# Thirty-two conditioning tiles of a two-layer block: loaded and multiplied in layer 1 instead of layer 0

## The chip, the core and the metric

The kernel runs on one core of a Trainium2 chip. The metric is the device time of one execution in microseconds, and lower is better. Five engines each work through their own instructions in order: TensorE (PE in the profile; PEld is its weight loads), VectorE (DVE), ScalarE (ACT), GpSimd (POOL) and SyncE (SP, which here only issues DMAs).

## What is computed

A block of two layers works on 1024 latent rows and 256 context rows of width 1024. Each layer has a token mixer (an HGRN recurrence, a windowed attention and an RG-LRU, side by side) and a convolved FFN. Each layer is conditioned by six vectors of 1024: shift, scale and gate of the mixer and of the FFN. They come from one matrix product per layer, and this product is what the change moves:

```python
for layer in range(DEPTH):
    want_ctx = layer < DEPTH - 1
    mod = sc @ ada_w[layer] + ada_b[layer]
    mod_c = scc @ ada_w[layer] + ada_b[layer]
    sh1, sc1, g1, sh2, sc2, g2 = jnp.split(mod, 6, axis=-1)
    ...
    h_l = modulate(x, norm_mix_g[layer], sh1, sc1)
    y_l, y_c = token_mixer(h_l, h_c, w_in[layer], w_out[layer], ...)
    x = x + g1[:, None, :] * y_l
    x = x + g2[:, None, :] * conv_ffn(modulate(x, norm_ffn_g[layer], sh2, sc2), ...)
```

So `sh1` and `sc1` of layer 1 are needed before that layer's mixer starts, while its other four vectors are needed only after the mixer.

## The kernel before

**Conditioning tiles.** `ada_w` of one layer is 1024 x 6144. `ada_gen(l, t)` (L183) makes one third of it, 2048 columns, in 16 tiles of 128 x 1024 (512 KB each). A tile is one load into a buffer named `aw` (L190, issued on SP) and four matmuls of 256 columns into the PSUM tile `ada` (L199). After the sixteenth tile, one copy on ACT (`adaev`, L205), four transposes (`adat`, L208) and two additions on DVE end the third. `ada_step` (L366) multiplies the tile that was loaded last and starts the load of the next. The third (0, 0) is made at the start; five thirds, 80 tiles, stand in a list and are made one tile at a time beside other work. A tile's buffer is taken from the weight rings named in `aring`: `wd`, or `wd` and `wr` in turn. Each of these two rings has a single buffer.

**Where the steps stand.** In layer 0 every projection of the mixer (`proj`, L557) has two steps, one behind each half of the latent rows: 16 projections, 32 tiles. Layer 0's attention (`att_step`, L1065) has 20 more. The remaining 28 stand in layer 0's FFN: `up` (L1260; its matmuls are `pu` for the latent rows, `puc` for the context rows) loads one ahead of each of its column tiles and multiplies it behind. Layer 1 has none.

**Weights of a projection.** `load_w` (L321) loads 512 KB into the single buffer of `wr` (L325), then ACT casts the high part (`wh`, L315) and DVE subtracts to get the low part (`wl`, L316); `wh` and `wl` have two buffers each. A projection is 48 matmuls of 512 columns into `pl` and, where context rows are wanted, 24 of 256 columns into `pc` (both L341).

**The HGRN stage.** For each of two head pairs, `hg_in` makes three projections and `hg_scan` (L638) works through groups of rows. Layer 1 reads out two groups, of 512 rows each, per scan. A group takes one score step and seven levels; each level copies operands on ACT (`ks` L690, `qz` L663), runs eight score matmuls (`hd`, L668; sixteen records in the trace), merges them on DVE (L692), and updates `Q` and `K` on DVE (L703, L705). Behind the levels stand `ho` (L719), transposes `kt` (L728, copied by ACT in L729), `kv` (L736), a chain on DVE over the chunks (L754) and `hi` (L765). Then come the readout `hg_out` with its normalization (L235 to L238, logarithm and exponential on ACT), the gates (`gs`, a sigmoid on ACT, L781) and the RG-LRU (`pg`, L833). The attention follows, with its queries and keys (`rot`, `q`), scores (`sc`) and so on.

**What sets the order.** The code is written stage after stage, but a scheduler lays out every engine's order from dependencies, priorities and free buffers when the program is built. A projection of a later stage can thus be laid between the instructions of an earlier one as soon as its weights have a buffer.

Of the kernel before, what the change touches and what calls it, by code (L numbers as in the profile page):

```python
# [87 lines left out]
def tile_dit(ctx: ExitStack, tc: tile.TileContext, x, c, ctxt, c_ctx, ada_w, ada_b, norm_mix_g, norm_ffn_g,  # L88
# [262 lines left out]
    adas = []  # L351
# [14 lines left out]
    def ada_step():  # L366

        ada_mm()
        ada_load()
# [91 lines left out]
        aring[1] += 1  # L461
        return wtile(aring[0][aring[1] % len(aring[0])], "aw", F32, 1)

    adas += [ada_gen(l_, t_, ada_tile) for l_, t_ in ((0, 1), (0, 2), (1, 0), (1, 1), (1, 2))]
    porder = InOrder(tc, POOL_ENGINE)
    with porder:
        G.tensor_copy(out=tiny("pj", [P, 1], 1), in_=last_raw[:, 0, 0:1])
# [82 lines left out]
    def mixers(l, hl, hc, steps):  # L550
# [6 lines left out]
        def proj(srcs, lat=True, cx=True):  # L557
            wh, wl = pre.pop() if pre else load_w(*srcs)
            pl = pc = None
            if lat:  # L560
                pl = ps("pl")
                for b in (B0, B1):
                    mm3(pl[:, b], wh, wl, *cut(hl, b))
                    ada_step()
            if cx:
                pc = pb1("pc")[:, 0:C]
                mm3(pc, wh, wl, *cut(hc, BC))
            return pl, pc
# [69 lines left out]
        def hg_scan(p, F2, K2, qp):  # L638
# [9 lines left out]
            for g in (1, 2, 0):  # L648
# [34 lines left out]
                Tm = f2  # L683
                m = 1
                for li in range(7):
                    nm_ = w // m
                    nb = nm_ // 2
                    if hasq and m < 64:
# [85 lines left out]
        def hg_gate(p):  # L774

            pl, pc = pr(O_G + p * P, cx=want)
            gsl = L("gs")
            gs = [X("gsc") if want else None, gsl[:, B0], gsl[:, B1]]
            for o_, a in zip(gs, (pc, pl[:, B0], pl[:, B1])):
                if a is not None:  # L780
                    S.activation(out=o_, in_=a, func=AF.Sigmoid)  # L781
                    V.scalar_tensor_tensor(out=o_, in0=a, scalar=rows["hn"][:, 2 * l + p:2 * l + p + 1], in1=o_, op0=mult, op1=mult)
            return gs
# [103 lines left out]
        def act(**kw):  # L887
            with order:
                S.activation(**kw)

        lrus = [lru(p) for p in range(2)]
        oSs = [hg_scan(0, *hg_in(0))]
        gin = hg_in(1)
        gate = hg_gate(0)
        oSs.append(hg_scan(1, *gin))
        gate = [gate, hg_gate(1)]
        hg_out(0, gate[0])
        hg_out(1, gate[1])
        for st in "c0 g0 c1 k0 s0 y0 o0 g1 k1 s1 y1 o1".split():
# [165 lines left out]
        def att_step(s_):  # L1065
# [14 lines left out]
                    done.add((qb, kv))  # L1080
            if pvs and pvs[0][0] <= s_:
                att_pv(*pvs.pop(0)[1:])
            if l == 0 and s_ % 2 and s_ < 4 * len(grp) - 40:
                ada_step()

        outs = []
# [33 lines left out]
            s_ += 1  # L1120
        ada_mm()
        aring[0] = ["wd"]
        if l == 0:
            ada_fin(0, 1)
        for i_, a in yr.items():
            hi, lo = L("yah", F32R), L("yal", F32R)
            split(hi, lo, a)
# [576 lines left out]
    for l in range(DEPTH):  # L1704
# [32 lines left out]
            sums7(xl, tb, n1)  # L1737
        next(f_)
        if want:
            for w_ in range(2):  # L1740
                ada_fin(1, w_)

            def after(si, xa):
                for mh, th in {1: [(0, 0)], 4: [(1, 1)], 5: [(1, 0)], 6: [(0, 1)]}.get(si, []):
# [53 lines left out]
```

## Time and profile before

| | |
|---|---|
| median of 3 runs | 3042.76 us (3041.82 to 3046.66) |
| profiled execution, its own time | 3040.61 us |
| its span, first to last instruction | 3038.8 us |
| PE busy | 2880.4 us, 95% |
| DVE, ACT, POOL busy | 1901.4, 1421.5, 236.6 us |
| tile `ada`, matmul records | 768 (96 tiles, 8 each) |
| granted clock, mean | 0.978 |

Times of the trace count from the first instruction. Layer 0's HGRN stage begins near 145 us, its attention near 490, its output projection at 669, its FFN at 789. Layer 1 begins near 1720 us; its first scan runs from 1812 to 1867 us, its second from 1895 to 1957, its attention from 2078 to about 2230. A busy PE means that one of its matmuls is in flight; it does not mean that all its columns do work.

### The profile page before, as it was taken

What the parts mean: (1) busy time and instruction counts of PE and PEld (TensorE: products, weight loads), DVE (VectorE), ACT (ScalarE), POOL (GpSimd) and SP (SyncE); (2) the same over time, 40 slices, a digit from 0 to 9 for tenths busy, and PEclk for the clock granted to TensorE, in tenths of its full rate; (3) what the DMA queues carried; (4) which work ended last, traced back from release to release, by engine and by line L of the source; (5) the groups of instructions that cost most, each with busy time, mean ns of one, the idle gap of its engine ahead of it and who ended that gap; (6) DMA issues with size and microseconds to landing.
All of it is one profiled execution on the core that took longest, in us unless ns stands there. A gap on an engine that the chain in (4) does not pass through costs nothing.

```text
span 3038.8 us, 41813 instructions
## 1 busy us (share of the span) xinstructions
PE 2880.4 (95%) x16208; PEld 2275.7 (75%) x16208; DVE 1901.4 (63%) x3005; ACT 1421.5 (47%) x2445; POOL 236.6 (8%) x348
## 2 busy tenths in 40 slices
PE   6999898999999999999999899998998999998998
PEld 5867676558888888888878787675666788876776
DVE  5466556665644434444676756767747777776876
ACT  5366764663422222222334545785745545544343
POOL 2000002000000000000101000002010111112010
PEclk9999999999999999999999999999998899999998
DMA  7211246423333223222476200114053333336762
GB/s 296 69 60 53 67 132 187 115 98 121 96 100 102 87 96 94 72 71 82 175 249 174 93 28 22 36 63 108 11 170 91 79 95 97 97 95 220 239 188 90
DMA packets 286678, 335.75 MB, mean 110 GB/s; under 512 B 19180, under 2 KB 211856, under 8 KB 286480
## 3 DMA queue, kind: packets, MB, share of 16 engines
q1 hardware_dynamic: 242928, 231.29, 24.6%
q0 software_dynamic: 43376, 101.73, 11.2%
q8 instruction: 128, 2.10, 0.3%
q14 instruction: 70, 0.57, 0.1%
q10 hardware_dynamic: 176, 0.07, 0.0%
HBM read 276.65 MB, written 56.36 MB: 110 GB/s over the span
## 4 chain that ended last, share of the span: by engine, by line
PE 76%; DVE 8%; ACT 7%; DMA 6%; issue 2%; SPq 0%; POOL 0%; ACTq 0%; DVEq 0%; POOLq 0%
PE pu L341 16%; PE pl L341 9%; PE ux L1445 8%; PE px L1651 5%; PE py L1651 4%; PE puc L341 4%; PE uz L1445 3%; PE iv L587 3%; PE yo L1160 3%; PE sc L1005 3%; PE yo L1154 2%; DMA raw<-in_ffn_w_down_dram 2%; PE pov L1047 2%; PE pt L1030 2%; PE pc L341 2%
## 5 line engine op out<-in xcount | busy, mean ns | idle before, releaser
L1445 PE MATMUL ux<-t,sw 128*128 128x512 f32 x1320 | 320.6, 399 | 20.1 <-ACT t L315 10.5
L1445 PEld LDWEIGHTS ux<-t,sw 128*128 128x128 f32 x1320 | 248.3, 190 | 85.3 <-ACT t L315 13.1
L341 PE MATMUL pu<-hh,wh 128*128 128x512 f32 x704 | 278.7, 396 | 0.1
L341 PE MATMUL pu<-hh,wl 128*128 128x512 f32 x704 | 276.3, 393 | 0.0
L341 PE MATMUL pu<-hl,wh 128*128 128x512 f32 x704 | 275.1, 391 | 0.0
L1278 DVE SCALAR_TENSOR_TENSOR u<-pu,col_fcb,u 128x1023 f32<-128x1023 f32 x44 | 56.3, 1282 | 324.5 <-ACT u L1277 324.5
L315 ACT CAST wh<-wr 128x1024 fp32r<-128x1024 f32 x110 | 115.2, 1049 | 227.7 <-PE pc L341 66.5
L341 PE MATMUL pl<-hh,wh 128*128 128x512 f32 x512 | 210.4, 411 | 2.2 <-ACT wh L315 0.9
L341 PE MATMUL pl<-hh,wl 128*128 128x512 f32 x512 | 205.2, 401 | 1.0 <-DVE wl L316 1.0
L341 PE MATMUL pl<-hl,wh 128*128 128x512 f32 x512 | 204.8, 400 | 0.0
L1277 ACT ACTIVATE u<-pu,col_nf,col_fcw 128x1024 f32<-128x1024 f32 x44 | 53.0, 1206 | 318.0 <-PE pu L341 318.0
L316 DVE TENSOR_TENSOR wl<-wr,wh 128x1024 fp32r<-128x1024 f32 x110 | 135.9, 1236 | 67.4 <-ACT wh L315 61.9
L315 ACT CAST ah<-raw 128x512 fp32r<-128x512 f32 x132 | 76.2, 619 | 200.2 <-PE py L1651 99.9
L341 PEld LDWEIGHTS pu<-hh,wh 128*128 128x128 f32 x704 | 132.2, 188 | 38.3 <-issue 11.4
L341 PEld LDWEIGHTS pu<-hh,wl 128*128 128x128 f32 x704 | 132.3, 188 | 29.0 <-issue 0.4
L341 PEld LDWEIGHTS pu<-hl,wh 128*128 128x128 f32 x704 | 132.2, 188 | 28.0 <-issue 0.2
L1445 PE MATMUL uz<-t,sw 128*128 128x512 f32 x528 | 132.6, 398 | 0.0
L341 PEld LDWEIGHTS pl<-hh,wh 128*128 128x128 f32 x512 | 96.1, 188 | 35.3 <-issue 14.0
L1445 PEld LDWEIGHTS uz<-t,sw 128*128 128x128 f32 x528 | 100.6, 191 | 23.4 <-ACT t L315 0.9
L1011 DVE TENSOR_REDUCE st<-sc 128x1 f32<-128x641 f32 (+2 forms) x144 | 106.7, 745 | 17.8 <-ACT sc L1010 16.3
L1014 ACT ACTIVATE pb<-sc,st 128x641 f32<-128x641 f32 (+2 forms) x144 | 106.3, 739 | 20.7 <-DVE st L1011 18.0
L341 PEld LDWEIGHTS pl<-hh,wl 128*128 128x128 f32 x512 | 96.2, 188 | 26.1 <-issue 5.1
(464 smaller groups left out, 7357.3 us busy)
## 6 DMA issues: line engine op xcount, KB each, us to landing
raw<-in_ffn_w_down_dram SPq DMA_DIRECT2D x220, 256.0 KB
aw<-in_ada_w_dram SPq DMA_DIRECT2D x96, 512.0 KB
wr<-in_ffn_w_up_dram SPq DMA_DIRECT2D x44, 512.0 KB
b<-act POOLq DMA_DIRECT2D x35, 512.0 KB, 8.0
wr<-in_w_in_dram SPq DMA_DIRECT2D x34, 512.0 KB
act<-u POOLq DMA_DIRECT2D x66, 256.0 KB, 3.5
wr<-in_w_out_dram SPq DMA_DIRECT2D x128, 128.0 KB
dr<-in_ffn_w_down_dram SPq DMA_DIRECT2D x22, 512.0 KB
```

What stands on the lines that cost most here:

```text
L315: S.copy(out=hi, in_=raw)
L316: eng.tensor_tensor(out=lo, in0=raw, in1=hi.bitcast(F32), op=sub)
L341: PE.matmul(out=o, lhsT=wl[k] if pi == 2 else wh[k], rhs=hl[k] if pi == 1 else hh[k], start=(k == 0 and pi == 0), stop=(k == nk - 1 and pi ...
L587: PE.matmul(out=po[:, 0:384], lhsT=hh[1 if pi == 1 else 0][k][:, t0:t0 + P], rhs=wiv[k][1 if pi == 2 else 0], start=(k == 0 and pi == 0), ...
L1005: PE.matmul(out=o_, lhsT=qt[:, hh, :], rhs=k_[:, ksl], start=(pi == 0), stop=(pi == 1 and not ms))
L1011: V.tensor_reduce(out=st[:, 0, c_], in_=sc[:, s0:769], axis=mybir.AxisListType.X, op=ALU.min)
L1014: S.activation(out=pb, in_=sc[:, s0:769], func=AF.Exp, bias=st[:, 0, c_], scale=-1.0, accum_out=st[:, 1, c_])
L1030: PE.transpose(out=pt[:, hh * P:(hh + 1) * P], in_=pbs[qb, kv][hh][:, i * P:(i + 1) * P], identity=ident)
L1047: PE.matmul(out=pov[hsl(v_), :], lhsT=vt(kbs[i])[:, hsl(v_)], rhs=ptss[qb][i][:, v_, :], start=(i == 0), stop=(i == nk - 1))
L1160: PE.matmul(out=o, lhsT=wl[k] if pi == 2 else wh[k], rhs=a[1 if pi == 1 else 0][:, s_], start=False, stop=(ki == 3 and pi == 2), skip_grou ...
L1445: PE.matmul(out=out, lhsT=(al if pi == 2 else ah)[:, k * P:(k + 1) * P], rhs=rhs[k][1 if pi == 1 else 0], start=(i in (1, 2, 7) and k == 0 ...
L1651: PE.matmul(out=acc[m], lhsT=(al if pi == 2 else ah)[:, i, c_], rhs=(bl if pi == 1 else bh)[:, i, :], start=((isy or si == 0) and j == 0 a ...
```

## The change

The list of the conditioning thirds loses (1, 1) and (1, 2), the 32 tiles for layer 1's mixer gate and FFN. They are put on it again when layer 1's mixer starts. Layer 1 gets steps at two places: ahead of each of the seven levels of a group that is read out (two scans of two groups: 28 steps, with both rings `wd` and `wr` for the tiles), and in the attention, where layer 1 now has a step in every second `att_step`. The projections of layer 1 still have none. The scales that belong to (1, 1) and (1, 2) are formed at the end of layer 1's attention instead of behind layer 0's FFN. Nothing else is edited.

```diff
--- before.py
+++ after.py
@@ -461,7 +461,7 @@
         aring[1] += 1
         return wtile(aring[0][aring[1] % len(aring[0])], "aw", F32, 1)
 
-    adas += [ada_gen(l_, t_, ada_tile) for l_, t_ in ((0, 1), (0, 2), (1, 0), (1, 1), (1, 2))]
+    adas += [ada_gen(l_, t_, ada_tile) for l_, t_ in ((0, 1), (0, 2), (1, 0))]
     porder = InOrder(tc, POOL_ENGINE)
     with porder:
         G.tensor_copy(out=tiny("pj", [P, 1], 1), in_=last_raw[:, 0, 0:1])
@@ -561,7 +561,8 @@
                 pl = ps("pl")
                 for b in (B0, B1):
                     mm3(pl[:, b], wh, wl, *cut(hl, b))
-                    ada_step()
+                    if l == 0:
+                        ada_step()
             if cx:
                 pc = pb1("pc")[:, 0:C]
                 mm3(pc, wh, wl, *cut(hc, BC))
@@ -683,6 +684,8 @@
                 Tm = f2
                 m = 1
                 for li in range(7):
+                    if l and hasq:
+                        ada_step()
                     nm_ = w // m
                     nb = nm_ // 2
                     if hasq and m < 64:
@@ -888,12 +891,16 @@
             with order:
                 S.activation(**kw)
 
+        if l:
+            adas.extend(ada_gen(1, t_, ada_tile) for t_ in (1, 2))
+            aring[0] = ["wd", "wr"]
         lrus = [lru(p) for p in range(2)]
         oSs = [hg_scan(0, *hg_in(0))]
         gin = hg_in(1)
         gate = hg_gate(0)
         oSs.append(hg_scan(1, *gin))
         gate = [gate, hg_gate(1)]
+        aring[0] = ["wd"]
         hg_out(0, gate[0])
         hg_out(1, gate[1])
         for st in "c0 g0 c1 k0 s0 y0 o0 g1 k1 s1 y1 o1".split():
@@ -1080,7 +1087,7 @@
                     done.add((qb, kv))
             if pvs and pvs[0][0] <= s_:
                 att_pv(*pvs.pop(0)[1:])
-            if l == 0 and s_ % 2 and s_ < 4 * len(grp) - 40:
+            if s_ % 2 and s_ < 4 * len(grp) - (1 - l) * 40:
                 ada_step()
 
         outs = []
@@ -1120,8 +1127,7 @@
             s_ += 1
         ada_mm()
         aring[0] = ["wd"]
-        if l == 0:
-            ada_fin(0, 1)
+        ada_fin(l, 1)
         for i_, a in yr.items():
             hi, lo = L("yah", F32R), L("yal", F32R)
             split(hi, lo, a)
@@ -1737,8 +1743,7 @@
             sums7(xl, tb, n1)
         next(f_)
         if want:
-            for w_ in range(2):
-                ada_fin(1, w_)
+            ada_fin(1, 0)
 
             def after(si, xa):
                 for mh, th in {1: [(0, 0)], 4: [(1, 1)], 5: [(1, 0)], 6: [(0, 1)]}.get(si, []):
```

Three places show how the laid-out orders differ (line numbers of the changed kernel are one to four higher in these stages). The first is PE in the first scan of layer 1, through the levels of its second group; `hd` are a level's scores, `pl` the matmuls of the next head pair's projections, `ada` the conditioning tiles. Before:

```order
L668 MATMUL hd<-qz,ks 64x128 x8
L341 MATMUL pl<-hh_14101,wh 128x512
L341 MATMUL pl<-hl_14109,wh 128x512
L341 MATMUL pl<-hh_14101,wl 128x512
L341 MATMUL pl<-hh_14102,wh 128x512
L668 MATMUL hd<-qz,ks 64x128 x8
L341 MATMUL pl<-hl_14110,wh 128x512
L341 MATMUL pl<-hh_14102,wl 128x512
L341 MATMUL pl<-hh_14095,wh 128x512
L341 MATMUL pl<-hl_14103,wh 128x512
L668 MATMUL hd<-qz,ks 64x128 x8
```

And now:

```order
L669 MATMUL hd<-qz,ks 64x128 x8
L199 MATMUL ada<-aw,cl 32x256
L669 MATMUL hd<-qz,ks 64x128 x8
L199 MATMUL ada<-aw,cl 32x256 x4
L669 MATMUL hd<-qz,ks 64x128 x8
L199 MATMUL ada<-aw,cl 32x256 x3
L669 MATMUL hd<-qz,ks 64x128 x8
L199 MATMUL ada<-aw,cl 32x256 x4
L669 MATMUL hd<-qz,ks 64x128 x8
L199 MATMUL ada<-aw,cl 32x256 x4
L669 MATMUL hd<-qz,ks 64x128 x8
L199 MATMUL ada<-aw,cl 32x256 x4
```

The three to five projection matmuls between two levels are gone, and up to four matmuls of a conditioning tile stand there. Over the whole first scan, 20 matmuls of `pl` stood ahead of the first `hd` and 76 between there and the second group's `ho`; now none stand in either place, and 15 stand in the scan's tail behind `kt`. Between the last `hi` of the first scan and the first `hd` of the second there were 96 of `pl` and 45 of `pc`; now there are 177 and 48. Up to the last `hi` of the second scan there were 113 of `pl`; now there are 26, of which 9 between its levels. Of the 32 tiles 14 are multiplied in the first scan, 15 in the second, one in the RG-LRU and two among the query projections.

The second place is SP in the same stage, from the projections of the first head pair on (`wr` are a projection's weights, `aw` conditioning tiles, `wg` small weights of the RG-LRU). Before:

```order
L325 DMA wr<-in_w_in_dram 128x8x128
L883 DMA wg<-in_lru_w_r_dram 64x2x64 x4
L883 DMA wg<-in_lru_w_i_dram 64x2x64 x4
L325 DMA wr<-in_w_in_dram 128x8x128 x13
L905 DMA cst<-const_cs_dram 128x1024
L906 DMA snt<-const_cs_dram 128x1024
```

And now:

```order
L325 DMA wr<-in_w_in_dram 128x8x128
L190 DMA aw<-in_ada_w_dram 128x1024 x13
L325 DMA wr<-in_w_in_dram 128x8x128
L190 DMA aw<-in_ada_w_dram 128x1024
L325 DMA wr<-in_w_in_dram 128x8x128 x3
L190 DMA aw<-in_ada_w_dram 128x1024 x13
L325 DMA wr<-in_w_in_dram 128x8x128
L190 DMA aw<-in_ada_w_dram 128x1024 x2
L325 DMA wr<-in_w_in_dram 128x8x128 x4
```

Thirteen projection loads stood in a row; now the loads of a whole scan's tiles stand ahead of the next projection's. The third place is ACT behind the second scan (`ST` is the scan's state, `gs` the second gate, `rr` the normalization). Before:

```order
L740 COPY STc<-kv 128x64
L740 COPY ST<-kv 128x64
L781 ACTIVATE gs<-pl 128x512
L235 ACT_TABLE_LOAD
L740 COPY ST<-kv 128x64
L740 COPY STc<-kv 128x64
L814 ACTIVATE lxc<-pl,col_nf 128x1024
L236 ACTIVATE rr<-pm_16308,epsc 128x512
L793 ACTIVATE o_16320<-oS 128x512
L237 ACTIVATE rr<-rr 128x512
L235 ACT_TABLE_LOAD
L238 ACTIVATE o_16305<-rr 128x512
```

And now:

```order
L235 ACT_TABLE_LOAD
L743 COPY ST<-kv 128x64
L743 COPY STc<-kv 128x64
L315 CAST wh<-wr 128x1024
L784 ACT_TABLE_LOAD
L784 ACTIVATE gs<-pl 128x512
L236 ACT_TABLE_LOAD
L236 ACTIVATE rr<-pm_16268,epsc 128x512
L784 ACT_TABLE_LOAD
L784 ACTIVATE gs<-pl 128x512
L237 ACT_TABLE_LOAD
L237 ACTIVATE rr<-rr 128x512
```

Both sigmoids of the second gate stood ahead of the first table load of the normalization; now the normalization has begun between them, and each needs a table load of its own. From here to the attention ACT has 16 table loads, and had 12; in the program 50, and had 46.

## Rows read from the trace of the kernel before

**Rows 1.** The page: span, TensorE's busy time, the chain by engine.

```profile
span 3038.8 us, 41813 instructions
...
PE 76%; DVE 8%; ACT 7%; DMA 6%; issue 2%; SPq 0%; POOL 0%; ACTq 0%; DVEq 0%; POOLq 0%
```

**Rows 2.** Stretches, all engines: length, busy us (instructions) per engine, clock, DMA share, GB/s.

```profile
900.00:950.00 50.00, 50.00 (x294) 42.40 (x294) 21.09 (x29) 12.24 (x15) 1.61 (x3) 1.00 0.28 90
...
1812.40:1866.60 54.20, 51.79 (x524) 38.76 (x524) 36.83 (x78) 33.57 (x59) 0.00 (x0) 0.97 0.02 5
...
1894.90:1956.70 61.80, 59.80 (x560) 43.19 (x559) 46.97 (x90) 45.55 (x76) 0.00 (x0) 1.00 0.06 18
...
1956.70:2037.10 80.40, 79.79 (x352) 60.58 (x351) 59.94 (x71) 65.29 (x91) 4.55 (x7) 1.00 0.21 68
...
2097.50:2118.00 20.50, 15.76 (x121) 12.49 (x120) 17.56 (x39) 15.42 (x47) 2.29 (x5) 1.00 0.45 128
```

**Rows 3.** Stretches, tile `ada` alone: length, PE, PEld (and ACT) busy, then as Rows 2.

```profile
789.00:840.00 51.00, 2.53 (x24) 0.60 (x24) 0.00 (x0) 1.00 0.25 77
...
840.00:1240.00 400.00, 15.97 (x200) 3.93 (x200) 0.58 (x1) 1.00 0.30 94
```

**Rows 4.** Timeline of PE, layer 0's FFN: start us, us, instruction.

```profile
886.62 0.64 PE L199 MATMUL ada<-aw,cl 128*32 128x256 f32 x8
...
887.19 0.51 PE L341 MATMUL pu<-hh,wh 128*128 128x512 f32 x1
...
901.79 0.50 PE L341 MATMUL pu<-hh,wh 128*128 128x512 f32 x1
...
1257.18 0.40 PE L341 MATMUL pu<-hh,wh 128*128 128x512 f32 x1
...
1270.90 0.39 PE L341 MATMUL pu<-hh,wh 128*128 128x512 f32 x1
```

**Rows 5.** Timeline of PE, layer 0's attention.

```profile
568.43 0.64 PE L199 MATMUL ada<-aw,cl 128*32 128x256 f32 x8
...
569.00 0.50 PE L1005 MATMUL sc<-kc,qt 128*128 128x256 f32 x2
```

**Rows 6.** Timeline, layer 1, first scan: PE, ACT and DVE through one level.

```profile
1842.73 0.85 PEld L668 LDWEIGHTS hd<-qz,ks 128*64 128x64 f32 x16 [0.36 <-ACT qz L663]
...
1843.42 1.26 ACT L663 COPY qz<-Q 64x512 f32<-64x512 f32 x2 [0.81 <-DVE Q L703]
...
1844.72 0.69 DVE L703 TENSOR_TENSOR Q<-Q,Tn 128x512 f32<-128x512 f32 x1
...
1844.88 0.85 PEld L668 LDWEIGHTS hd<-qz,ks 128*64 128x64 f32 x16 [0.37 <-ACT qz L663]
```

**Rows 7.** Stretches, tile `pl` alone: length, PE, PEld, DVE, ACT busy, then as Rows 2.

```profile
1807.80:1812.40 4.60, 4.58 (x20) 3.41 (x19) 1.50 (x2) 1.19 (x2) 1.00 0.24 69
...
1812.40:1854.00 41.60, 22.19 (x76) 13.02 (x76) 0.00 (x0) 0.00 (x0) 1.00 0.02 6
...
1866.60:1894.90 28.30, 22.19 (x96) 17.95 (x96) 1.50 (x2) 5.40 (x10) 1.00 0.20 56
...
1894.90:1940.80 45.90, 26.15 (x94) 16.14 (x93) 1.49 (x2) 1.19 (x2) 1.00 0.09 24
...
1940.80:1956.70 15.90, 5.93 (x19) 3.10 (x18) 5.33 (x5) 2.47 (x3) 1.00 0.00 1
```

**Rows 8.** Timeline, layer 0: a tile's load issued on SP, its matmuls on PE.

```profile
466.18 0.56 SPq L190 DMA_DIRECT2D aw<-in_ada_w_dram  x1
...
470.66 0.64 PE L199 MATMUL ada<-aw,cl 128*32 128x256 f32 x8 [1.16 <-DMA aw<-in_ada_w_dram]
```

**Rows 9.** Timeline, layer 1, end of the first scan: ACT, then PE.

```profile
1855.13 0.59 ACT L722 COPY oS<-ho 128x512 f32<-128x512 f32 x1 [1.43 <-PE ho L719]
...
1860.69 0.43 PE L765 MATMUL hi<-Q,ST 64*64 64x128 f32 x4 [1.03 <-DVE ST L754]
```

**Rows 10.** Groups of ACT's instructions, 1940 to 1970 us: count, busy us, mean ns, idle before.

```profile
L235 ACT ACT_TABLE_LOAD x4 | 5.1, 1283 | 0.1
```

## The prediction

> **What bounds the kernel now.** I read the page first. The span is 3038.8 us, and the chain that ended last lies on TensorE for 76% of it [rows 1]. TensorE is called busy 95% of the time, so the next view is the stretches: does it set the pace where the change takes work away, and where it puts it? In layer 0's FFN it does: it is busy for all of 50.00 us, DVE and ACT for 21.09 and 12.24 [rows 2]. In layer 1's two scans it is called busy too, 51.79 of 54.20 and 59.80 of 61.80 us [rows 2], but the timeline shows another pace-setter. One level lasts 2.15 us (1842.73 to 1844.88); its scores wait for ACT's `qz` copies, which wait for DVE's `Q` [rows 6]. TensorE is full there because it works on projections in the meantime: 76 matmuls of `pl` fill 22.19 of the 41.60 us of the first scan's levels, 94 fill 26.15 of 45.90 in the second [rows 7]. So those matmuls ride along nearly free. From the second scan to the attention TensorE is the bound again, 79.79 of 80.40 us [rows 2].
>
> The whole question is therefore: the change puts conditioning tiles into gaps that already hold other work. What happens to that work?
>
> All sums are against the profiled execution (own time 3040.61 us); the median is 2.15 us above it, and the last step adds that.
>
> **Part 1, what leaves layer 0.** By the order, 28 tiles leave the FFN and 4 the attention. The FFN's tiles are 24 and 200 records [rows 3], eight to a tile, so 28. A column tile with one lasts 14.60 us (887.19 to 901.79), one without lasts 13.71 (1257.18 to 1270.90) [rows 4]: 0.89 us each, though the multiplication itself lasts 0.64 and its successor starts 0.57 after it [rows 4]. TensorE is the bound, so this comes off the end: 28 x 0.89 = **24.9 us**; the lower bound is 28 x 0.57 = 16.0. In the attention one tile moves the next scores by 0.57 us (568.43 to 569.00) [rows 5]: 4 x 0.57 = **2.3 us**. The loads that go with them (30% of the DMA engines' time in that FFN stretch [rows 3]) were waited for nowhere I can see, so I give their absence nothing. Gain: 27.2 us.
>
> **Part 2, the first scan and what follows.** The tiles take their buffers from `wr`, too, the single buffer that the next projections' weights need. SP issues thirteen tile loads in a row where thirteen projection loads stood; the second weight load waits behind them, and so do its cast, its subtraction and its matmuls. By the order 20 + 76 = 96 matmuls leave the time from the last query projection to the scan's tail; 15 come into the tail and 81 go behind the scan, where TensorE is the bound. Behind the scan 96 such matmuls took 22.19 us [rows 7], 0.231 us each: 81 x 0.231 = **18.7 us**. Terms beside it:
> - The 15 in the tail are 3.5 us of work. TensorE's idle time in the whole scan is 54.20 - 51.79 = 2.4 us [rows 2], 1.03 of it in the tail's wait for `ST` [rows 9]; I choose 1.7 as the tail's. I take the difference, **1.8 us** (0 to 3.5).
> - ACT's cast of a projection weight now stands ahead of the tail's copies, and waits for a load that waits for the last tile in that buffer. In the trace those copies start at 1855.13 with nothing between [rows 9]. A load issued at 466.18 was used at 470.66, 4.48 us later [rows 8]; most of that should pass while the last levels run. I take **1.2 us** (0 to 2.5).
> - The tiles themselves. A load, once issued, takes 4.48 us to its use, plus 0.64 for the matmuls [rows 8]. Two buffers give a tile every (4.48 + 0.64) / 2 = 2.56 us, while a level lasts 2.15 [rows 6]. Seven tiles in seven levels could thus be 0.4 us late each, 14 x 0.4 = 5.7; the loads run ahead through the score step, and not every tile stands in a chain. I take **2 us** (0 to 5).
> - Without projections in between, scores start at once. The scores' wait ends with ACT, not with a matmul of `pl` [rows 6], so I take nothing (0 to -2).
>
> Loss of part 2: 18.7 + 1.8 + 1.2 + 2 = 23.7 us.
>
> **Part 3, the second scan up to the attention.** The second scan had 94 + 19 = 113 matmuls of `pl` in 61.8 us [rows 7]; by the order 26 remain and 87 go behind: 87 x 0.231 = **20.1 us**, since TensorE is full there [rows 2]. Against this the second scan's levels took 45.90 us where the first's took 41.60 [rows 7], with the same chain and more projection work between. Its tail took 15.9 us where the first's took 12.6 (1854.0 to 1866.6) [rows 2, 7]. I give back those 4.3 us, and of the tail's 3.3, whose cause I don't see, 1.0: **-5.3 us** (0 to -8). Late tiles again **2 us** (0 to 5). ACT gets four more table loads of 1.283 us [rows 10], 5.1 us; ACT is busy 65.29 of the 80.40 us behind the scan [rows 2], so I put half on the path: **2.5 us** (0 to 5.1). Two or three tiles come behind the scans, where TensorE is full: **1.2 us**. In layer 1's attention nothing waits for a tile; TensorE has 4.7 us of 20.5 free [rows 2]. The scales of the moved thirds are formed there; I cost them at nothing, for they lie beside a stage with room; uncovered they would be a few DVE instructions of under a microsecond. Loss of part 3: 20.1 - 5.3 + 2 + 2.5 + 1.2 = 20.5 us.
>
> **The sum.** 23.7 + 20.5 - 27.2 = +17.0 us, 3057.6 us on the profiled execution; 2.15 more for the median is 3059.8, about **3060 us**. With every gain large and every loss small (18.7 - 2 + 20.1 - 8 + 1.2 - 27.2 = 2.8) it is near 3046; the other way round (81 + 87 matmuls 38.8, terms 3.5, 2.5, 5, 5, 5.1, 1.2, against 16.0 + 2.3) about +43, near 3085.
>
> The table loads are the one term where a page would change the sum. The rows show 1283 ns for one [rows 10], and only the load. The Trainium skill, "ScalarE: Activation LUTs", on what a table load costs, adds a drain of the pipeline ahead of it, and puts a switch at about 2.66 us. By that the four would be 10.6 us of ACT instead of 5.1, and half of it on the path would make the total 2.8 us higher; the trace shows 0.1 us of idle time ahead of the four loads [rows 10], which speaks against it here.
>
> **Rivals.**
> (a) About the same. The scans themselves come out shorter, by 8 us each and not 5.3 in one alone, because TensorE now answers each `qz` at once, and no tile is late. For it: the second scan's levels are 4.3 us longer than the first's with the same chain [rows 7]. Against it: the scores wait for ACT by the trace [rows 6]. The sum loses 8 (first scan), 2.7 (second) and 4 (tiles): 17.0 - 14.7 = +2.3, near 3045 us.
>
> (b) Faster: the projections are absorbed behind the scans. What is called a full TensorE there may not be: its weight loads are busy 60.58 of 80.40 us (0.75), and 38.76 of 54.20 (0.72) in the first scan, against 42.40 of 50.00 (0.85) in the FFN [rows 2]. If the moved 38.8 us run in that slack, the loss shrinks while the gain stands. To break even 17.0 of the 38.8 us must be absorbed, 44%; at the ratio of 0.75 to 0.85 only 12% would be. If 28 us are, the total is -11 us, near 3032. Against it: 79.79 of 80.40 us with 352 matmuls is 0.228 us each, the price of 0.231 that `pl` has alone [rows 2, 7]; I see no room.
> The Trainium skill, "Perfetto Trace Analysis", in its section on the most contended engine, says that matmul busy time is a bad measure and that the weight loads' busy share is a good one. By that rule this rival would have its slack; the equal price per matmul is why I give it little.
>
> (c) Much slower: TensorE's clock falls in the scans. The granted clock is 0.97 and 1.00 there now, that is 2.4 GHz, with TensorE full [rows 2]. Afterwards it works some 0.85 us of scores (by its weight loads [rows 6]) and 0.64 of a tile in a level of 2.15. At 1.2 GHz these 1.5 us become 3.0, and as the scores' 0.85 lies on the level's chain, each level grows by 0.85, or by 1.4 when the tile's is in the way too: over 28 levels 24 to 39 us. If half of the levels are hit, +20, near 3080 us. Against it: in the attention TensorE is busy only 15.76 of 20.50 us, at a clock of 1.00 [rows 2].
> The Trainium skill, "TensorE: Matmul & The Clock Gate", in its section on oscillation, tells that waits between short bursts of matmuls throttle the engine again and again; no row here shows a scan without filler.
>
> **How the numbers follow.** The forecast, slower by 6 to 30 us, has 0.72; (a) 0.11; (b) 0.07; (c) 0.10. Measurements of this kernel can tell about 0.2%, 6 us, from no change: faster 0.07, same 0.11, slower 0.82. The range takes in the forecast's own spread, the lower end to the edge of (a), 3045, and the upper, 3073, where several bounds are high at once; (b) and most of (c) stay out.
>
> **What would show it.** In the profile of after: column tiles of layer 0's FFN all near 13.7 us, and layer 1's mixer begun about 27 us earlier. In the first scan of layer 1 TensorE's busy time falls well below the 51.79 us, with idle time released by ACT `qz`; a level stays near 2.1 us. SP's second `wr` load comes behind the tile loads. From the last `hi` of the first scan to the first `hd` of the second the time grows by some 19 us, and from the second scan to the attention by about as much. If levels are clearly below 2.0 us, (a) is right; if the stretch behind the second scan does not grow, (b); if the clock in the scans reads near 0.5, (c). What would make the number wrong most easily is how late a tile is, which no row of before shows for tiles in the scans.

## The result, and the profile after

The changed kernel took 3059.67 us (median; 3055.66 to 3066.05), the kernel before, measured beside it, 3044.71. The ratio is 1.0054, with an interval of 1.0044 to 1.0065: some 16 us slower. The profiled execution has a span of 3053.9 us, 15.1 more than before.

The page of the changed kernel, its span and the chain by engine (compare [rows 1]):

```profile
span 3053.9 us, 41829 instructions
...
PE 77%; DVE 7%; DMA 6%; ACT 6%; issue 2%; POOL 0%; SPq 0%; ACTq 0%; DVEq 0%; POOLq 0%
```

The chain looks the same. Where the 15 us are is seen only when the same events are compared in both traces. Each row of this table runs from the first or last instruction of one tile on TensorE to that of the next, in us:

| stretch | before | after | difference | forecast |
|---|---|---|---|---|
| start to layer 0's first `sc` | 489.25 | 489.97 | +0.7 | 0 |
| layer 0's attention, to the first `yo` | 179.72 | 175.02 | -4.7 | -2.3 |
| output projection, to the first `pu` | 120.20 | 119.27 | -0.9 | 0 |
| FFN up, to the first `px` | 693.06 | 669.77 | -23.3 | -24.9 |
| FFN down, to layer 1's first `iv` | 239.36 | 237.14 | -2.2 | 0 |
| mixer of layer 1, to the first `hd` | 90.85 | 89.81 | -1.0 | |
| first scan, to the end of the last `hi` | 54.16 | 56.40 | +2.2 | |
| from there to the second scan's first `hd` | 28.30 | 46.09 | +17.8 | these three: +23.7 |
| second scan | 61.82 | 61.90 | +0.1 | |
| from its end to the first `rot` | 80.41 | 101.94 | +21.5 | |
| to the first `sc` | 40.87 | 44.46 | +3.6 | |
| layer 1's attention, to the first `yo` | 144.93 | 147.07 | +2.1 | these four: +20.5 |
| from there to the end of the span | 815.87 | 815.06 | -0.8 | 0 |

Layer 0 gains 30 us, layer 1 gives back 46. These are one trace each, and traces spread. Seven kernels of the experiments below and this one run the same TensorE order up to layer 1's first `iv`; their leads over the kernel before at that point lie between 24.8 and 30.4 us, 26.9 on average, and the changed kernel's is the largest. So differences of one to three us in layer 0 may be spread. Around the scans the traces repeat better: experiments 1, 5 and 6, which have the old order there, take 61.8 us for the second scan and 80.4 to `rot`, as the kernel before.

The timeline of TensorE in layer 0's FFN shows a column tile's first matmul and the next one's:

```profile
879.17 0.39 PE L341 MATMUL pu<-hh,wh 128*128 128x512 f32 x1
...
892.88 0.39 PE L341 MATMUL pu<-hh,wh 128*128 128x512 f32 x1
```

That is 13.71 us, the period without a conditioning tile [rows 4], at a place where the kernel before had one. In layer 1, the four stretches of the table around the scans (length, then busy us and instructions of PE, PEld, DVE, ACT and POOL, granted clock, DMA share, GB/s):

```profile
1781.00:1837.40 56.40, 44.26 (x572) 30.09 (x572) 39.01 (x80) 35.38 (x61) 0.00 (x0) 0.97 0.50 150
...
1837.40:1883.50 46.10, 46.10 (x227) 38.54 (x227) 12.38 (x23) 10.77 (x20) 0.00 (x0) 1.00 0.08 24
...
1883.50:1945.40 61.90, 47.54 (x596) 32.39 (x595) 43.62 (x87) 40.56 (x69) 0.00 (x0) 0.97 0.47 145
...
1945.40:2047.30 101.90, 101.82 (x446) 76.94 (x447) 68.37 (x80) 79.02 (x107) 4.54 (x7) 1.00 0.20 63
```

Compared with [rows 2], the scans keep their length (56.40 and 61.90 us), but TensorE is busy 44.26 and 47.54 us in them instead of 51.79 and 59.80. The two stretches behind them are full of TensorE's work (46.10 of 46.10, 101.82 of 101.90) and longer by 17.8 and 21.5 us. SP's part of the timeline shows what keeps the projections out (start, time from the first issue to the end of the last, operation, count):

```profile
1785.47 31.89 SPq L190 DMA_DIRECT2D aw<-in_ada_w_dram  x12
...
1819.62 0.38 SPq L325 DMA_DIRECT2D wr<-in_w_in_dram  x1
```

Twelve tile loads are issued from 1785.47 on, each as its buffer comes free, and the next projection's weights (`wr`) only at 1819.62, when the first scan is at its second group's last levels. In the trace of the kernel before, no tile load stands among the weight loads of this stage, and the first of the four below went out ahead of the first scan's start at 1812.4:

```profile
1799.81 78.17 SPq L325 DMA_DIRECT2D wr<-in_w_in_dram  x4
```

A level with its tile, in the timeline of PE, ACT and DVE:

```profile
1790.23 1.09 PE L669 MATMUL hd<-qz,ks 128*64 128x128 f32 x16
...
1791.26 0.64 PE L199 MATMUL ada<-aw,cl 128*32 128x256 f32 x8
...
1791.35 1.26 ACT L664 COPY qz<-Q 64x512 f32<-64x512 f32 x2 [0.42 <-DVE Q L706]
...
1792.66 1.09 PE L669 MATMUL hd<-qz,ks 128*64 128x128 f32 x16 [0.76 <-ACT qz L664]
...
1793.75 0.64 PE L199 MATMUL ada<-aw,cl 128*32 128x256 f32 x8
```

From one `hd` to the next it is 2.43 us here; the scores still wait for ACT's `qz`, as in [rows 6]. But now some tiles are waited for, too. The `ada` matmuls of both scans, and TensorE's idle time ahead of them:

```profile
L199 PE MATMUL ada<-aw,cl x232: 379/379/404, 1784.8 to 1929.2; 128*32 128x256 f32 x116
...
  DMA aw<-in_ada_w_dram: 13.1, 15
```

13.1 us of idle time, yet the scans are only 2.2 and 0.1 us longer: most of those waits must lie in time in which TensorE would have waited for `qz` anyway.

### The profile page after: what moved, and what is told of

The parts are those of the page before. It is cut to its first block, busy times and chain, and to the rows that moved or that the text cites. A ratio compares the mean times of both kernels' runs of the same rounds, so it can differ in the third digit from the quotient of the medians.

```text
span 3053.9 us, 41829 instructions
## 1 busy us (share of the span) xinstructions
PE 2870.3 (94%) x16208; PEld 2276.6 (75%) x16208; DVE 1899.8 (62%) x3005; ACT 1426.6 (47%) x2449; POOL 237.9 (8%) x348
## 4 chain that ended last, share of the span: by engine, by line
PE 77%; DVE 7%; DMA 6%; ACT 6%; issue 2%; POOL 0%; SPq 0%; ACTq 0%; DVEq 0%; POOLq 0%
PE pu L341 16%; PE pl L341 9%; PE ux L1451 9%; PE px L1657 5%; PE py L1657 4%; PE puc L341 4%; PE uz L1451 3%; PE iv L588 3%; PE sc L1012 3%; PE yo L1166 3%; PE yo L1160 2%; PE pov L1054 2%; PE pt L1037 2%; PE pc L341 2%; PE pd L1259 2%
## 5 line engine op out<-in xcount | busy, mean ns | idle before, releaser
L1451 PEld LDWEIGHTS ux<-t,sw 128*128 128x128 f32 x1320 | 248.1, 190 | 84.1 <-ACT t L315 13.1
```

The lines of the kernel that those rows point to most:

```text
L1451: PE.matmul(out=out, lhsT=(al if pi == 2 else ah)[:, k * P:(k + 1) * P], rhs=rhs[k][1 if pi == 1 else 0], start=(i in (1, 2, 7) and k == 0 ...
```

## The experiments

All were timed in five rounds beside the kernel before; a difference in us below is the ratio's distance from 1 times 3044.6 (3043.0 for the last two). "The changed kernel" is the one of the result. A price per tile from the times is uncertain by about 0.17 us (the intervals of two ratios over 32 tiles), and one from two traces by about 0.1 (the spread of 3 us above).

**1. No moved tiles at all.**

```diff
-            adas.extend(ada_gen(1, t_, ada_tile) for t_ in (1, 2))
+            V.memset(mod[1][:, 16:48, :], 0.0)
```

> The changed kernel without the 32 moved tiles at all: layer 1's last four conditioning vectors are left zero, nothing of them is loaded or multiplied, and the matmuls of TensorE in layer 1's two scans stand as in the kernel before. It measures what leaving layer 0 gives by itself. Theory (the sum's part 1): 27.2 us faster than before, 23 to 31; on the trace layer 1's first score would start about 30 us earlier and nothing would be lost after it. Rival (part of the gain is given back later whatever is done in the scans): under 20 us faster, with the lead shrinking somewhere after the scans.

Measured: 3019.28 us, ratio 0.9921 (0.9908 to 0.9935), 24 us faster (20 to 28). So the gain of layer 0 is real, and the 27.2 of the sum lies within the interval. The trace gives the terms: FFN up 22.4 us shorter than before, 0.80 us a tile, and layer 0's attention 5.8 us shorter for four tiles. The lead at layer 1's first `hd` is 24.7 us, and 23.6 at `ux` behind its attention: nothing is given back in the scans. (This trace has the smallest lead of the eight kernels with the same layer 0.)

**2. No tiles, but the weight buffer held through the scans.** The tiles are taken out as in experiment 1, the steps in the scans too, and the tile `hold` is put in:

```diff
+            if l:
+                hold = wtile("wr", "aw", F32, 1)
+                V.memset(hold[:, 0:1], 0.0)
             for g in (1, 2, 0):
...
                     S.copy(out=oS[g], in_=po[:, 0:w])
+                    if l and g == 2:
+                        V.tensor_copy(out=hold[:, 0:1], in_=oS[g][:, 0:1])
```

> The same without tiles, but the buffer of the projection weights is held through the levels of both of layer 1's scans by an otherwise unused tile (one small write ahead, one small write at the end). So the projections are kept out of the scans, and no tile is loaded, waited for or multiplied there. Theory (what costs is the projections that no longer fill the scans): some 190 matmuls move behind the scans at 0.231 us, 44 us, less what the scans get shorter (forecast 5, bounds 0 to 10): 34 to 44 us slower than the one without the hold, so about 5 to 15 us slower than before. Rival 1 (the tiles themselves cost, by being late and by standing between the scores): at most 10 us slower than without the hold. Rival 2 (the scans shorten much without fill): levels of clearly under 2.0 us, total loss of 20 to 30 us. Rival 3 (the clock falls when TensorE works only half of a level): granted clock near 0.5 in the scans and a loss of over 50 us.

Measured: 3060.23 us, ratio 1.0055 (1.0042 to 1.0067): 41 us slower than without the hold and as slow as the changed kernel, without a single tile. Its two scans and the two stretches behind them (columns as above):

```profile
1784.70:1842.60 57.90, 41.06 (x453) 32.79 (x454) 37.91 (x80) 35.47 (x61) 0.00 (x0) 0.79 0.07 19
...
1842.60:1890.60 48.00, 48.00 (x234) 40.13 (x234) 15.45 (x28) 12.63 (x23) 0.00 (x0) 1.00 0.08 23
...
1890.60:1952.80 62.20, 43.93 (x451) 35.16 (x450) 40.48 (x83) 41.15 (x70) 0.00 (x0) 0.73 0.06 18
...
1952.80:2058.00 105.20, 105.20 (x459) 80.90 (x460) 67.44 (x80) 76.47 (x104) 5.01 (x7) 1.00 0.21 65
```

The two stretches are full of TensorE's work and 48.0 and 105.2 us long, against 28.4 and 80.4 in experiment 1: 44.5 us more. By the order 89 and 107 matmuls of `pl` have moved behind the scans, 196 x 0.231 = 45.3. The first rival falls, since no tile is left to cost anything. That the time equals the changed kernel's is in part chance: here 28 matmuls more have moved than by the changed kernel's order (81 + 87), while the changed kernel loses more in its attention. The second rival falls as well: the scans are not shorter without the projections but some longer, 57.9 and 62.2 us.

The third rival is half right. The granted clock is 0.79 and 0.73 in these scans: between the scores' bursts TensorE waits, and a part of the scores runs at 1.2 GHz. Three bursts in a row in the timeline of the first scan (PE, PEld and ACT):

```profile
1789.84 1.09 PE L672 MATMUL hd<-qz,ks 128*64 128x128 f32 x16 [1.30 <-ACT qz L667]
...
1791.91 1.57 PEld L672 LDWEIGHTS hd<-qz,ks 128*64 128x64 f32 x16 [1.22 <-ACT qz L667]
...
1792.67 1.26 ACT L667 COPY qz<-Q 64x512 f32<-64x512 f32 x2
...
1793.98 1.36 PEld L672 LDWEIGHTS hd<-qz,ks 128*64 128x64 f32 x16 [0.50 <-ACT qz L667]
```

The sixteen matmuls of the first burst take 1.09 us, as in the changed kernel's level above; in the next two the weight loads alone take 1.57 and 1.36 us, instead of 0.85 in [rows 6]. Yet the bursts start at 1789.84, 1791.91 and 1793.98, 2.07 us apart each time: ACT's next `qz` copy begins at 1792.67, in the middle of the slow burst, so in these bursts most of what the scores lose lies beside it. Of all 512 score matmuls 269 lasted over 350 ns here, none in the kernel before and 47 in the changed one. With all of it the two scans are 5.8 us longer than in experiment 1 (52.5 and 61.8 us there) and 4.1 longer than in the kernel before. That is neither the loss of over 50 us that the rival here asked nor the 24 to 39 of the prediction's rival (c), or half of that for half of the scores.

**3. All loads, fewer of the multiplications.**

```diff
-            for q in range(4):
+            for q in range(4 if l == 0 or t == 0 or i in (0, 1, 14, 15) else 1):
```

> The changed kernel with one matmul of four for each moved tile (the others of the 32 tiles are left out, so those four vectors are incomplete); every load, its buffer and its place stay. Theory (the occupied weight buffer is what costs): within 0 to 8 us of the changed kernel, on the fast side, so 8 to 16 us slower than before. Rival (the multiplications in the scans cost): 14 to 20 us faster than the changed kernel, 32 x 0.64 x 3/4 = 15.

Measured: 3060.84 us, ratio 1.0055 (1.0042 to 1.0067), the changed kernel's within the interval. This is what the theory said, but it does not decide against the rival. The edit keeps one matmul of four in 24 of the 32 tiles only; the other 8 keep all four. And it hardly takes work from TensorE, as a tile with one matmul (two records) shows beside the 0.64 us of four:

```profile
1795.24 0.62 PE L199 MATMUL ada<-aw,cl 128*32 128x256 f32 x2
```

The four matmuls of a tile start within 0.02 us of one another and run side by side. So TensorE is busy with tiles for 19.2 us in the two scans, against 20.0 in the changed kernel, and the 15 us that the rival counted were never taken away. That the multiplications cost little in the emptied scans is seen elsewhere: the changed kernel's scans, with 29 tiles in them, are 2.2 and 0.1 us longer than before. What the time is lost to, the occupied weight buffer and not the tiles, rests on experiments 2 and 4.

**4. Tiles in the scans, from the other ring only.**

```diff
             adas.extend(ada_gen(1, t_, ada_tile) for t_ in (1, 2))
-            aring[0] = ["wd", "wr"]
+            aring[0] = ["wd"]
```

> The changed kernel with the steps in the scans kept, but the tiles take their buffer from one ring only, the one that the projections do not use. By the order 58 and 80 projection matmuls stand in the levels of the two scans again (70 and 87 before, none and 2 in the changed kernel), with 9 and 11 tiles beside them. Theory (the shared buffer is what costs): most of the 44 us come back; what is left is TensorE's time for the tiles, 29 x 0.6 = 17, less a few us of idle time: 10 to 20 us faster than before. Rival (steps in the scans cost wherever their buffer is from): no faster than before, since one buffer at some 5 us a tile is later still.

Measured: 3032.84 us, ratio 0.9958 (0.9944 to 0.9971), 13 us faster than before and 29 us faster than the changed kernel, by one word. The same four stretches:

```profile
1785.94:1845.31 59.37, 58.09 (x619) 39.09 (x619) 37.59 (x78) 33.47 (x59) 0.00 (x0) 1.00 0.36 106
...
1845.31:1874.39 29.08, 29.08 (x152) 24.02 (x151) 13.85 (x25) 11.91 (x22) 0.00 (x0) 1.00 0.27 80
...
1874.39:1943.57 69.18, 68.14 (x670) 45.53 (x669) 49.63 (x95) 47.86 (x80) 0.00 (x0) 1.00 0.40 123
...
1943.57:2024.72 81.15, 81.08 (x356) 61.59 (x357) 58.30 (x70) 65.78 (x92) 4.69 (x7) 1.00 0.21 67
```

TensorE is full in all of them, the scans included (58.09 of 59.37 and 68.14 of 69.18 us). The stretches behind the scans are back at 29.08 and 81.15 us; the scans are 6.9 and 7.4 us longer than in experiment 1, with 12 and 14 tiles multiplied in them and their tails. So by the trace a tile costs some 0.55 us in a scan that holds projections: TensorE's time for it, and no more. The times give 0.35 us for each of all 32 tiles.

**5 and 6. Tiles in layer 1's attention only,** one in every second step, and one in every step (`-` and `+` of the second in the last lines):

```diff
-                    if l and hasq:
-                        ada_step()
...
-            aring[0] = ["wd", "wr"]
+            aring[0] = ["wd"]
...
-            if s_ % 2 and s_ < 4 * len(grp) - (1 - l) * 40:
+            if (l or s_ % 2) and s_ < 4 * len(grp) - (1 - l) * 40:
```

> No steps in the scans: all 32 tiles are made in layer 1's attention, one in every second of its steps. The scans are as in the kernel before. Theory (a tile costs about 0.6 us wherever TensorE is full, and nothing where it waits): layer 0's gain of about 25 us, less 32 x 0.57 = 18 us, plus some 5 us for the tiles that fall into the attention's start, where TensorE waits: 12 us faster than before, 5 to 20. Rival (in an attention a tile costs 1.2 us, as the four that left layer 0's attention gave back about 5 us): 25 - 38 = 13 us slower than before.

> As the one before, but a tile in every step of layer 1's attention until all 32 are made, so more of them fall into its first 45 us, where TensorE waits (some 10 us of idle time). Theory: 32 tiles less what 10 us of idle time take up, 15 x 0.6 to 20 x 0.6: 13 to 18 us faster than before. Rival (their loads, 512 KB each at twice the rate, come late or slow the others there): slower than the run with every second step.

Measured: 3048.0 us, ratio 1.0010 (1.0001 to 1.0018), and 3048.15 us, ratio 1.0013 (1.0005 to 1.0022). For the first, neither the theory (12 us faster) nor its rival (13 slower) holds; for the second the theory (13 to 18 us faster) fails, and its rival does not show either, since the two kernels are as fast as each other. The 32 tiles cost 27 and 28 us against experiment 1, 0.85 to 0.88 each. 80 us of the attention with a tile in every second step, then the same stretch without tiles (experiment 1):

```profile
2100.00:2180.00 80.00, 78.36 (x562) 44.16 (x559) 52.20 (x108) 51.91 (x136) 2.12 (x4) 1.00 0.38 114
```

```profile
2100.00:2180.00 80.00, 78.80 (x521) 48.45 (x519) 61.03 (x129) 59.65 (x163) 1.59 (x3) 1.00 0.04 11
```

TensorE is busy 78.36 and 78.80 us of 80: the idle time that I counted on (4.7 of 20.5 us [rows 2]) lies in the attention's first 45 us or so, and behind them TensorE is nearly full. That a tile costs 0.85 there and 0.55 among projections isn't explained by its matmuls, which last 0.64 us in both; the order of the attention's own matmuls changes with the tiles, and I did not separate the two.

**7. Tiles behind the projections of layer 1, from one ring.**

```diff
-                    if l == 0:
-                        ada_step()
+                    ada_step()
...
-                    if l and hasq:
-                        ada_step()
...
-            aring[0] = ["wd", "wr"]
+            aring[0] = ["wd"]
```

> The 32 tiles stand behind the halves of layer 1's projections, from one ring. By the order 16 of them are multiplied behind the second scan among projections, 5 between the scans, 6 in the levels and the rest ahead. TensorE is full at nearly all of these places. Theory: 32 x 0.6 to 0.83 us = 19 to 27 us against the gain of about 25: 6 us faster to 2 us slower than before. Rival (the buffer decides, not TensorE's time): as fast as with all tiles from one ring in the scans or faster, 12 to 20 us faster than before.

Measured: 3030.32 us, ratio 0.9954 (0.9942 to 0.9967), 14 us faster than before: better than I expected, and as good as experiment 4, as the rival said. The trace puts the price at 0.48 us a tile (from layer 1's `iv` to `ux`, 618.1 us, against 602.8 in experiment 1, over 32 tiles); the times put it at 0.31, with an interval of 0.17 to either side. I had taken 0.6 to 0.83; that price failed, and the rival's range holds. That TensorE's time does not count, as the rival has it, is not shown: by both a tile has its price.

**8. Tiles from the general pool of buffers.**

```diff
-        return wtile(aring[0][aring[1] % len(aring[0])], "aw", F32, 1)
+        r_ = aring[0][aring[1] % len(aring[0])]
+        return L("aw") if r_ == "h4" else wtile(r_, "aw", F32, 1)
...
-            aring[0] = ["wd", "wr"]
+            aring[0] = ["h4"]
```

> The changed kernel, but the tiles of the scans and projections of layer 1 take their buffers from the general pool of 4 KB buffers, so neither ring of the weights is touched. By the order 41 and 96 projection matmuls stand in the levels (70 and 87 before, none and 2 in the changed kernel), 117 between the scans (96 before, 177 in the changed kernel). Theory (the projections must not wait for a buffer; a tile costs 0.6 us): gain 25, less 32 x 0.6 = 19, less 21 x 0.231 = 5 of moved projection, plus 4 of idle time: 5 us faster than before, 0 to 12. Rival (holding any buffer there costs as much): slower than before by 10 us or more.

Measured: 3040.62 us, ratio 0.9984 (0.9976 to 0.9993), 5 us faster than before, as expected: a price of 0.60 us a tile, the moved projections included. The price is not even, though: in the trace the first scan is as long as before with 13 tiles in it (54.1 us), and the second, with 16, takes 78.7 us instead of 61.8. What the second loses beyond TensorE's time for the tiles I did not separate.

**9 and 10. Layer 0's attention freed of tiles, too.** Experiment 7, and steps in layer 0's scans:

```diff
                 for li in range(7):
+                    if l == 0 and hasq and li % 2:
+                        ada_step()
```

In the second kernel the condition is `l == 0 and g and hasq and li % 3 == 1`.

> The tiles behind layer 1's projections as in the run before (one ring), and layer 0's 16 attention tiles moved too: every second level of layer 0's scans has a step, so that no attention and no FFN makes a tile. Price theory from the runs so far: a tile costs about 0.8 us in layer 0's FFN, 0.9 in an attention, 0.3 to 0.5 among projections and in scans whose weight buffer is left alone. So 16 x 0.4 to 0.6 us = 6 to 10 us less than with tiles behind layer 1's projections only: 20 to 25 us faster than before. Rival (layer 0's scans, where the projections have tiles of their own already, are full, and the tile's price there is that of the attention): 12 to 16 us faster than before, as without this step.

> The same with steps in two levels of each long group of layer 0's scans only; by the order 5 of the 16 tiles are left in layer 0's attention. Price theory: 11 x 0.4 to 0.6 = 4 to 7 us less than with layer 1's part alone, 18 to 21 us faster than before, between the two. Rival (full scans): no difference from layer 1's part alone, 12 to 16 us faster.

Measured: 3022.02 us, ratio 0.9931 (0.9919 to 0.9943), 21 us faster than before, the fastest complete kernel of this study and 37 us faster than the changed one; the tiles that left layer 0's attention (16) gave the 7 us more than experiment 7 that the price theory asked (2 to 12 by the two intervals). The second: 3033.4 us, ratio 0.9968 (0.9957 to 0.9979), 10 us faster than before (6 to 13): below what the theory said and below the rival's 12 to 16, whose lower end the interval just reaches, and no faster than experiment 7. Two stretches of it ahead of layer 0's attention, and TensorE's wait in the first:

```profile
490.00:500.00 10.00, 6.91 (x38) 3.66 (x40) 3.96 (x6) 1.26 (x2) 1.52 (x3) 0.90 0.91 229
...
500.00:510.00 10.00, 10.00 (x59) 8.32 (x52) 3.28 (x7) 3.50 (x9) 0.00 (x0) 0.75 0.60 163
...
498.74 1.93 PE L199 MATMUL ada<-aw,cl 128*32 128x256 f32 x16 [2.79 <-DMA aw<-in_ada_w_dram]
```

The tiles that were left for the end fell among the query projections, where the DMA engines were busy 0.91 of the time; one wait of 2.79 us for a tile holds up TensorE with the first scores behind it, and the clock falls to 0.75. By the first `sc` this kernel is 9.1 us behind experiment 9, by the first `yo` 11.8. How much of it is the waits, the clock and the tiles themselves I did not separate; the price theory has no place for the first two.

## Why the prediction was right, point by point

The time came out as forecast, and the cause is the one named: experiment 2 shows the loss without the tiles, and experiment 4 keeps tiles in the scans and takes the loss away. That 3059.67 came within 0.3 us of 3060 is luck. The kernel before was 2 us slower in this comparison than in the earlier runs that the forecast started from, so the change itself was 15 to 16 us and not 17; and by the table layer 0 gave 3.2 us more than forecast, part 2 lost 4.7 less, part 3 lost 6.8 more, and the rest of the span gave 0.8. The errors cancelled.

- **Part 1**, 27.2 us, was right in sum: experiment 1 gives 24 (20 to 28), and the eight traces with the same layer 0 a lead of 26.9 on average. The trace of the changed kernel has 23.3 for the FFN and 4.7 for the attention, experiment 1's 22.4 and 5.8. So the FFN term was over by 1.6 to 2.5 (a tile was worth 0.80 to 0.83, not 0.89: one pair of column tiles stood for all). The attention term was half of what the traces show; I had only counted the next scores' delay, 0.57, and experiments 5 and 6 put a tile in layer 1's attention at 0.85 to 0.88. The DMA share of 0.30 that I gave to the tiles' loads is that of all loads in the stretch: in the changed kernel the same 400 us have 0.20.
- **Part 2**, 23.7 us; the table shows 19.0. The main term was right: 18.7 for 81 matmuls, 17.8 measured. The surcharges for the cast, the tail and late tiles (5.0 together) were mostly not there: the first scan and its beginning came out 1.2 us longer in all.
- **Part 3**, 20.5 us; the table shows 27.3. Its main term, 20.1 us of `pl` and 1.2 of tiles, stands in the 21.5 us from the second scan to `rot`, and leaves nothing for the four table loads: ACT was not on the path there, TensorE was busy 101.82 of 101.90 us. The step that failed is the 5.3 us that the second scan was to give back. It did not get shorter (61.90 against 61.82): its tail lost 2.9 us with the projections gone from it, and its levels gained 3.0. I had read the second scan's longer levels [rows 7] as the projections' doing, "with the same chain"; experiment 2 shows 62.2 us without them. The larger part of the 4.3 us is another chain at the scan's start (timeline of PE and ACT, the kernel before):

```profile
1812.44 1.09 PE L668 MATMUL hd<-qz,kd 128*64 128x128 f32 x16
...
1814.49 1.09 PE L668 MATMUL hd<-qz,ks 128*64 128x128 f32 x16
...
1894.90 1.09 PE L668 MATMUL hd<-qz,kd 128*64 128x128 f32 x16
...
1895.78 0.59 ACT L781 ACTIVATE gs<-pl 128x512 f32<-128x512 f32 x1
...
1897.19 0.60 ACT L781 ACTIVATE gs<-pl 128x512 f32<-128x512 f32 x1 [0.31 <-DVE gs L782]
...
1897.79 1.73 ACT L663 COPY qz<-Q 64x512 f32<-64x512 f32 x2
...
1899.57 1.09 PE L668 MATMUL hd<-qz,ks 128*64 128x128 f32 x16
```

  From the score step (`kd`) to the first level's scores (`ks`) it is 2.05 us in the first scan and 4.67 in the second, where ACT makes the first head pair's gate (`gs`) ahead of the `qz` copies. The change left this gate in its place: the same distance is 4.51 us in the changed kernel and 3.89 in experiment 2. The other 1.7 us, at the second group, were not traced. As for the table loads, the drain that the prediction weighed does not show in the changed kernel, neither ahead of a load nor behind it; ACT goes on without a gap:

```profile
1952.78 0.60 ACT L784 ACTIVATE gs<-pl 128x512 f32<-128x512 f32 x1
1953.40 1.28 ACT L236 ACT_TABLE_LOAD   x1
1954.69 0.69 ACT L236 ACTIVATE rr<-pm,epsc 128x512 f32<-128x512 f32 x1
```

- **The attention**, costed at nothing, took 5.7 us more from `rot` to `yo`. The 20 us around its start show it:

```profile
2097.00:2107.00 10.00, 7.11 (x20) 3.96 (x20) 8.04 (x16) 4.41 (x14) 1.26 (x1) 0.66 0.44 96
...
2107.00:2117.00 10.00, 6.70 (x39) 5.07 (x39) 7.63 (x16) 6.67 (x19) 3.89 (x7) 0.83 0.98 253
```

  At the same distance from the first `sc` the kernel before has:

```profile
2083.20:2093.20 10.00, 4.16 (x20) 2.44 (x20) 9.03 (x18) 5.53 (x15) 1.49 (x1) 1.00 0.57 117
2093.20:2103.20 10.00, 8.32 (x51) 6.46 (x52) 7.99 (x18) 6.65 (x20) 3.77 (x7) 0.83 0.89 239
```

  A clock of 0.83 and a high DMA share in the second stretch are thus nothing new. New are the clock of 0.66 in the first, where the same twenty matmuls take 7.11 us instead of 4.16, and two late tiles among the query projections ahead of it. Without any tile, from `rot` to `yo`, experiment 2 took 183.9 us, experiment 1 188.2 and the kernel before 185.8, against 191.5 here; so the excess is 3 to 8 us, by what one compares with. Which of clock, loads and tiles took how much is open.
- **Rival (a)**, shorter scans: ruled out by experiment 2. **Rival (b)**, projections absorbed behind the scans: ruled out by the same two stretches, where 196 moved matmuls cost 44.5 us, 0.227 each, the price that 79.79 us for 352 matmuls gave before [rows 2]. The Trainium skill's page "Perfetto Trace Analysis", in the section on identifying the most-contended engine, judges TensorE's headroom by the busy share of its weight loads (and by the FLOPs done, which I did not work out), and by that rule there was slack at 0.75 [rows 2]; the stretches of experiment 2 have 40.13 of 48.00 and 80.90 of 105.20 us of PEld, 0.84 and 0.77, and no slack at all. So here the price per matmul told more than either busy share.
- **Rival (c)**, the clock: it fell in the emptied scans of experiment 2, to 0.79 and 0.73, and this agrees in kind with the Trainium skill, "TensorE: Matmul & The Clock Gate", section on HAM oscillation: waits between short bursts throttle the engine. The page's waits are for DMA; here TensorE waited for ACT, 1.30, 1.22 and 0.50 us in the three rows shown. The rival's price was wrong: about half of the scores (243 of 512) stayed under 350 ns, and in the bursts shown a slow one runs beside the next `qz` copies instead of ahead of them. In the changed kernel, with tiles between the scores, it read 0.97.

## What to carry to other kernels

A gap that is already filled is not a gap: before putting work into a stage that waits for another engine, look at what the busy engine does in that wait, and count what will be pushed out, at its price where the engine is full. A prefetch that borrows a buffer of someone else's ring costs what the owner can no longer do early, and this can be more than the work itself: 41 us here, for tiles that cost at most 28 in any other place tried. The same work from the other ring, one word's difference, made the kernel faster than before instead of slower.

## What the runs showed of the hardware that I had not expected

- A fallen clock can cost little where another engine sets the pace: with the granted clock at 0.79 and 0.73 the two scans were 57.9 and 62.2 us long, and 54.2 and 61.8 us at 0.97 and 1.00 with 170 projection matmuls among their levels [rows 2, 7].
- Four matmuls of 32 columns of weights each, whose results go to four different groups of 32 partitions, last together hardly longer than one: 0.64 us for four, 0.62 for one (experiment 3). Leaving three of the four out saved TensorE next to nothing (19.2 us instead of 20.0 in two scans).
- The same four matmuls, 0.64 us in the trace, cost 0.80 to 0.83 us in layer 0's FFN, 0.85 to 0.88 in layer 1's attention and, by times and traces, 0.3 to 0.55 among projections, with TensorE called busy at all three places.
